# A one-core decoder layer: the first query block by token, squares at other places, one column more in the last sum

## The chip, the cores and the metric

The kernel runs on one core of one Trainium2 chip. The time is device microseconds of one launch on that core; the kernel before has a median of 2016.69 us over three runs (2016.46 to 2019.35). Lower is better. Besides the times there is one profiled execution, with the start and the length of every instruction on TensorE (PE, and PEld for its weight loads), VectorE (DVE), ScalarE (ACT) and GpSimd (POOL), the instructions that the SP queue issues, and the DMA transfers.

## The reference, cut to what matters

One decoder layer over 256 tokens of width 2048 in float32: two token mixers (retention and a gated recurrence) merged by gates, an attention over 256 memory rows, a gated feed-forward part, and a final normalisation.

```python
def rmsnorm(x, w):
    return x * lax.rsqrt(jnp.mean(x * x, axis=-1, keepdims=True) + 1e-6) * w

hn = rmsnorm(x, norm_mix_w)
q, k, v, g_ret, xr, yr, g_a, g_b = jnp.split(hn @ w_in, offsets, axis=-1)   # q, k: 1024 columns, the others 2048
q = rotary(q.reshape(b, s, 8, 128), positions)                               # turned by the token's position
k = rotary(k.reshape(b, s, 8, 128), positions) * 128 ** -0.5
ret = silu(g_ret) * head_groupnorm(chunkwise_retention(q, k, v), ret_gn_w)
rnn = gelu(yr) * rg_lru(causal_dwconv(xr, ...), ...)
merged = sigmoid(g_a) * (ret @ w_proj_ret) + sigmoid(g_b) * (rnn @ w_proj_rnn)
h = x + merged @ w_mix_out
h = h + memory_cross_attention(rmsnorm(h, norm_xa_w), rmsnorm(mem, norm_mem_w), ...)
h = h + conv_gated_ffn(rmsnorm(h, norm_ffn_w), ...)
return rmsnorm(h, final_norm_w)
```

## The kernel before, in words

**Products.** Every float32 product is made from parts: an operand is rounded to a high part `hi` (type fp32r) and the rest is the low part `lo`. Three products are summed, high by high, low by high and high by low. The weights come from one stream in memory, laid out in the order of use, in chunks of four k-tiles (128 rows each) by 512 columns, 1 MB; the first chunks of the first two products are of two k-tiles (`EARLY`). `prefetch` (L233) issues a chunk's load from the SP queue into a buffer `raw` (L249), of which there are three (`RAW_BUFS`), casts it to `hi` on ScalarE (L276; for the very first chunk on VectorE, L274) and subtracts for `lo` on VectorE (L277). The parts have six buffers of two k-tiles each, so that three chunks can be ready. `chunks` (L289) asks for two chunks ahead and, after each chunk, runs the functions that `later(n, fn)` put down for n chunks on. All matmuls keep the order in which they are written; the other instructions of each engine are put into an order by a planner, from the order of the text, priorities and its own estimate of when data are there. At run time each engine and each queue goes through its order strictly, waiting where something is not there.

**By token and by feature.** `steps_n` (L352) makes a product by token: a piece of the activations (128 x 128, of `xs`) is held in TensorE, and 512 weight columns stream past; the result has tokens on the partitions. Where features must be on the partitions, `turned_rows` (L401) copies the result out of PSUM (`rows`), and `by_dma` (L377) splits the words into halves on ScalarE (`pl`, L385), turns them with two DMA transposes from SP (`pt`, L387) and joins the halves on ScalarE (`f`, L396), some chunks later. `steps_t` (L312) makes a product by feature at once, with the weight piece held and the activations streaming: 512 columns (high and low) past `hi`, 256 (high) past `lo`. Only the first query block is made this way, into two PSUM accumulators; `joined` (L412) adds the two halves of each accumulator, and `rotated` (L589) applies the rotary tables. The first query block (`q_steps`) and the first value block (`v_steps`) take turns, chunk by chunk.

**The rows of x.** `Pairs` loads x by feature in pieces of two k-tiles (`xt`, L530) and splits them (`s`, L451 and L452). `load_x` (L223) loads x by token (`nat`), for the sums of squares that `sum_squares` (L488) makes on ScalarE while the chunks 8 and 9 are prefetched.

**Residual stages.** `residual` (L840) runs the products with `w_mix_out` and with `xa_w_o` in four blocks of 512 columns. For the first two blocks three chunks each are run ahead. After each block the rows of h are updated (L852), the squares are summed on ScalarE (`squares`, L867) and the rows are turned with `by_dma` for the next stage. In the `w_mix_out` stage `memory_steps` (L871) adds, ahead of block 1, the sums of squares of all four blocks of memory rows (`mnat`, eight instructions on ScalarE, L493).

**The tail.** `last_down` (L1012) makes the last 512 columns of the result, for each half of the tokens (`tt`) in two parts of 256 columns. Each part is added to the row and squared with a sum (L1025). VectorE then adds up the other sums and eps (L1030, L1031), adds the last one (L510), GpSimd raises to the power -0.5 (L512), and VectorE and ScalarE scale the rows, which go out by DMA.

Of the kernel before, what the change touches and what calls it, by code (L numbers as in the profile page):

```python
# [9 lines left out]
F32 = mybir.dt.float32  # L10
# [25 lines left out]
URGENT = 5  # L36
# [102 lines left out]
def hybrid_layer(  # L139
# [93 lines left out]
    def prefetch(n):  # L233
        while len(ahead) < n and taken[0] < len(stream):
# [6 lines left out]
            raw = wp.tile([P, KC, BW], F32, tag="raw", bufs=RAW_BUFS, name=nm("raw"))  # L241
# [12 lines left out]
            if i >= 5:  # L254
                load_x(min(4, i - 4))
# [56 lines left out]
    def steps_t(w, row, st, nk, col):  # L312

        accs = [acc(), acc()]
        first = gemms[0] == 0
        phase = 0
        for k0, n, parts in chunks(nk, w, row, col):
            last = k0 + n >= nk
            tiles = [(kk, j) for j in range(2) for kk in range(n)]
            if first and k0 == 0:  # L320
                runs = [[(t, pr, kk, j) for t in (0, 1)] for kk in range(n) for pr in range(2) for j in range(2)]
            elif last:
                runs = [[(t, pr, kk, j) for kk, j in tiles] for pr in range(2) for t in (1 - pr, pr)]
            else:
                runs = [[(t, pr, kk, j) for pr in range(2) for kk, j in tiles] for t in (phase, 1 - phase)]
                phase = 1 - phase
            for i, run in enumerate(runs):
                for t, pr, kk, j in run:
                    k = k0 + kk
                    sx = st[k // 2][:, k % 2, :]  # L330
                    part = parts[kk // KH][t][:, kk % KH, (2 * pr + j) * P : (2 * pr + j + 1) * P]
                    a = accs[pr][:, j, :]
                    if t == 1:
                        a, sx = a[:, S:BW], sx[:, 0:S]
                    mm(
                        a, part, sx, start=k == 0 and t == 0, stop=k == nk - 1 and t == 0, skip_group_check=True
                    )
                if i + 1 == len(runs) // 2 and not last and not first and isinstance(st, Pairs):
                    st[(k0 + n) // 2 + 1]
            yield accs  # L340

    def gemm_t(*args):
        return ended(steps_t(*args))

    def products_n(o, sx, hi, lo, tt, start, stop):
        h = sx[:, tt * P : (tt + 1) * P]
        l = sx[:, S + tt * P : S + (tt + 1) * P]
        mm(o, h, hi, start=start, stop=False)
        mm(o, l, hi, start=False, stop=False)
        mm(o, h, lo, start=False, stop=stop)  # L350

    def steps_n(w, row, st, nk, col):  # L352

        a = acc()
        for k0, n, parts in chunks(nk, w, row, col):
            for tt in range(2):
                for kk in range(n):
                    k = k0 + kk
# [52 lines left out]

    def joined(a, s="j"):  # L412

        c = tmp("c")
        o = tmp(s)
        with tc.high_priority(URGENT):
            act.copy(c, a[:, :, S:BW])
            dve.tensor_tensor(out=o, in0=a[:, :, 0:S], in1=c, op=ALU.add)
        return o
# [121 lines left out]
    q_steps = steps_t("w_in", 0, xs, NT, O_Q)  # L541
# [41 lines left out]
    qjoin = [joined(t, "q") for t in next(q_steps)]  # L583
    assert next(q_steps, None) is None
# [87 lines left out]
    for g in range(2):  # L672
        dec = big([P, 4, S], s="dec")
        vs, turned = [], ([], [])
        for b, o in enumerate((O_Q, O_K)):
            if g + b:
                def rotate_both(f, o=turned[b]):
                    o.append(rotated(f[:, 0:2, :]))
                    later(0, lambda: o.append(rotated(f[:, 2:4, :])))
# [160 lines left out]
    def residual(w, st, out, wcol, steps=None):  # L840
# [3 lines left out]
        for b in range(4):  # L844
# [8 lines left out]
            squares(h, ss, b)  # L853
            by_dma(hrow[b], lambda f, b=b: turn(f, b, out, wcol))
# [157 lines left out]
    def last_down(b0, hid, n, b):  # L1012
        h = hrow[b]
        accs = [acc(), acc()]
        parts = [p for _, _, ps in chunks(n, "ffn_w_down", b0 * BW, b * BW) for p in ps]
        for tt in range(2):
            for c in range(2):
                cs = slice(c * S, (c + 1) * S)
                for k in range(n):
                    hi, lo = (t[:, k % KH, cs] for t in parts[k // KH])  # L1020
                    products_n(accs[c][:, tt, 0:S], hid[k // 2][:, k % 2, :], hi, lo, tt, k == 0, k == n - 1)
                y = h[:, tt, cs]
                dve.tensor_add(y, y, accs[c][:, tt, 0:S])
                junk = tp.tile([P, S], F32, tag="tr", bufs=2, name=nm("junk"))
                dve.scalar_tensor_tensor(  # L1025
                    out=junk, in0=y, scalar=1.0, in1=y, op0=ALU.mult, op1=ALU.mult,
                    accum_out=ss3[:, tt, b + c : b + c + 1],
                )
            part = sp_.tile([P, 1], F32, tag="pt3", bufs=2, name=nm("pt3"))
            dve.tensor_reduce(out=part, in_=ss3[:, tt, 0:4], axis=AX.X, op=ALU.add)  # L1030
            dve.tensor_scalar(out=part, in0=part, scalar1=1.0 / D, scalar2=EPS, op0=ALU.mult, op1=ALU.add)  # L1031
            r = rsqrt_small(ss3[:, tt, 4:5], 1, 1.0 / D, part)
            for c in (1, 0, 3, 2):
                y = hrow[c][:, tt, :]
                if c == 3:
                    dve.scalar_tensor_tensor(
                        out=y, in0=y, scalar=r, in1=wfin[1][:, 1, :], op0=ALU.mult, op1=ALU.mult
# [70 lines left out]
```

## Time and profile before

| what | value |
|---|---|
| median of three runs | 2016.69 us |
| the profiled execution's own time | 2016.58 us |
| its span | 2014.5 us |
| mean granted TensorE clock | 0.997 |
| TensorE busy | 1999.1 us |
| ScalarE, VectorE busy | 1247.8, 1263.5 us |
| GpSimd busy | 7.7 us |
| DMA, mean | 210 GB/s |
| TensorE idle, 60 us to the end, until `hi` | 2.5 us, once |
| the same, until `lo`, until `s` | 0.5 us, once each |

The span runs from the first to the last instruction of the trace; the time of the run has 2.08 us more. Matmuls are pipelined, so a single matmul of 512 columns is shown as 0.39 us long while the next one starts 0.227 us after it; intervals from start to start are read, not lengths. A line of the timeline that stands for several instructions shows their number (x16), the start of the first and the time to the end of the last. The granted clock in the windows is the share of full speed that TensorE was given.

### The profile page before, as it was taken

How to read it: one execution, taken by the hardware profiler on the slowest of the kernel's cores; microseconds unless marked ns; L12 is line 12 of the kernel's file. 1: busy time of each engine (PE TensorE's matmuls, PEld its weight loads, DVE VectorE, ACT ScalarE, POOL GpSimd, SP SyncE). 2: the span in 40 equal slices, each digit the busy share in tenths (PEclk: the TensorE clock that was granted, in tenths of full speed). 3: DMA queues.
4: the chain of work that ended last, by engine and by line, in shares of the span. 5: the costliest groups of instructions: out<-in, count | busy, mean ns of one | idle time of the engine just before them, and what ended most of it. 6: DMA issues, size and time to landing. Idle time of an engine off the chain costs nothing.

```text
span 2014.5 us, 23604 instructions
## 1 busy us (share of the span) xinstructions
PE 1999.1 (99%) x9044; PEld 1664.3 (83%) x9044; DVE 1263.5 (63%) x1563; ACT 1247.8 (62%) x1506; POOL 7.7 (0%) x12
## 2 busy tenths in 40 slices
PE   9999999999999999999999999999999999999998
PEld 7888888888888888878888888888888888888887
DVE  5867757888545555456555555566775577664675
ACT  5556648888444455487675656766763466744763
POOL 0000000000000000000000000000000000000000
PEclk9999999999999999999999999999999999999999
DMA  8755757665555566767766645767665566655663
GB/s 299 233 210 172 235 199 196 235 206 188 209 190 192 195 207 211 260 227 241 227 208 205 197 176 184 217 205 215 214 223 216 195 191 217 232 210 200 208 230 125
DMA packets 189376, 423.02 MB, mean 210 GB/s; under 512 B 131664, under 2 KB 136400, under 8 KB 144208
## 3 DMA queue, kind: packets, MB, share of 16 engines
q1 hardware_dynamic: 188832, 421.00, 63.5%
q8 instruction: 70, 1.15, 0.2%
q10 hardware_dynamic: 432, 0.53, 0.1%
q14 instruction: 42, 0.34, 0.0%
HBM read 388.46 MB, written 2.10 MB: 194 GB/s over the span
## 4 chain that ended last, share of the span: by engine, by line
PE 96%; DMA 1%; ACT 1%; issue 1%; DVE 1%; SPq 0%; POOLq 0%; POOL 0%; ACTq 0%; DVEq 0%
PE acc L214 94%; PE sm L214 3%; DMA raw<-in_wall 1%; DMA pt<-pl 1%; DVE lo L277 0%; ACT pl L385 0%; ACT hi L276 0%; ACT f L396 0%; ACT junk L867 0%; DVE nat L852 0%; ACT s L451 0%; SPq L249 0%; ACT nat L1042 0%; DVE s L452 0%; SPq L387 0%
## 5 line engine op out<-in xcount | busy, mean ns | idle before, releaser
L214 PE MATMUL acc<-hi,s 128*128 128x512 f32 (+1 forms) x5680 | 1739.9, 388 | 3.0 <-ACT hi L276 2.5
L277 DVE TENSOR_TENSOR lo<-raw,hi 128x1024 fp32r<-128x1024 f32 (+1 forms) x714 | 859.4, 1218 | 645.9 <-ACT hi L276 629.5
L214 PEld LDWEIGHTS acc<-hi,s 128*128 128x128 f32 x5680 | 1062.4, 188 | 220.1 <-ACT hi L276 2.9
L214 PE MATMUL acc<-lo,s 128*128 128x512 f32 (+1 forms) x2840 | 1100.6, 388 | 0.5 <-DVE lo L277 0.5
L276 ACT CAST hi<-raw 128x1024 fp32r<-128x1024 f32 (+1 forms) x712 | 733.0, 1048 | 497.5 <-PE acc L214 428.1
L214 PEld LDWEIGHTS acc<-lo,s 128*128 128x128 f32 x2840 | 533.7, 188 | 110.1 <-DVE lo L277 1.0
L396 ACT COPY f<-pt 128x1024 uint16<-128x1024 uint16 x118 | 151.4, 1349 | 85.0 <-DMA pt<-pl 85.0
L385 ACT COPY pl<-rows 128x1024 uint16<-128x1024 uint16 x90 | 89.7, 1044 | 64.5 <-DVE rows L409 55.8
L409 DVE TENSOR_SCALAR rows<-acc,ro 128x512 f32<-128x512 f32 x68 | 47.7, 742 | 3.1 <-PE acc L214 3.1
L965 DVE SCALAR_TENSOR_TENSOR fv<-f,pf,fv 128x255 f32<-128x255 f32 (+1 forms) x88 | 35.8, 477 | 0.7 <-ACT fv L963 0.7
L965 DVE SCALAR_TENSOR_TENSOR fg<-f,pf,fg 128x255 f32<-128x255 f32 (+1 forms) x88 | 35.6, 477 | 0.0
L452 DVE SCALAR_TENSOR_TENSOR s<-f,pb,s 128x256 fp32r<-128x256 f32 x48 | 20.1, 478 | 6.6 <-ACT s L451 6.6
L963 ACT ACTIVATE fv<-f,pf 128x256 f32<-128x256 f32 x44 | 22.9, 592 | 0.0
L963 ACT ACTIVATE fg<-f,pf 128x256 f32<-128x256 f32 x44 | 22.8, 591 | 0.0
L428 ACT ACTIVATE s<-fo 128x512 fp32r<-128x512 f32 x22 | 13.6, 633 | 14.2 <-DVE fo L985 14.2
L777 DVE SCALAR_TENSOR_TENSOR xr<-f,pa,xr 128x255 f32<-128x255 f32 (+2 forms) x48 | 19.9, 478 | 3.1 <-ACT xr L775 3.0
L451 ACT ACTIVATE s<-f,pb 128x256 fp32r<-128x256 f32 x48 | 20.6, 498 | 0.0
L385 ACT COPY pl<-nat 128x1024 uint16<-128x1024 uint16 x16 | 15.9, 1042 | 6.9 <-DVE nat L852 6.9
L214 PEld LDWEIGHTS sm<-s,s 128*128 128x128 f32 x144 | 18.8, 191 | 0.9
L214 PE MATMUL sm<-s,s 128*128 128x256 f32 (+1 forms) x144 | 18.6, 279 | 0.0
L214 PE MATMUL acc<-s,hi 128*128 128x512 f32 x64 | 17.4, 410 | 0.4 <-DVE hi L274 0.3
L440 ACT ACTIVATE v<-acc,ro 128x512 fp32r<-128x512 f32 x16 | 10.9, 683 | 7.7 <-DVE v L441 7.7
(152 smaller groups left out, 625.5 us busy)
## 6 DMA issues: line engine op xcount, KB each, us to landing
raw<-in_wall SPq DMA_DIRECT2D x352, 1024.0 KB, 4.8
nat<-in_x SPq DMA_DIRECT2D x8, 512.0 KB, 7.8
raw<-in_wall SPq DMA_DIRECT2D x6, 512.0 KB, 6.8
nat<-in_mem SPq DMA_DIRECT2D x4, 512.0 KB, 9.3
xt<-in_mem_t SPq DMA_DIRECT2D x8, 256.0 KB, 3.6
pt<-pl SPq DMA_TRANSPOSE x118, 4.1
xt<-in_x_t SPq DMA_DIRECT2D x7, 256.0 KB, 8.2
out<-nat SPq DMA_DIRECT2D x6, 256.0 KB, 2.8
```

Source lines behind the costliest of these rows:

```text
L214: tc.keep_in_program_order(pe.matmul(*a, **k))
L276: act.copy(hi[:, ds], raw[:, cs, :])
L277: dve.tensor_tensor(out=lo[:, ds], in0=raw[:, cs, :], in1=hi[:, ds].bitcast(F32), op=ALU.subtract)
L385: act.copy(planes[:, :, h, :], words[:, h])
L396: act.copy(halves_[:, h], turned_[:, h])
L409: dve.tensor_scalar_mul(rows[:, tt, :], a[:, tt, :], r[:, tt : tt + 1])
L428: act.mul(t[:, :, 0:S], src, scale)
L451: act.activation(t[:, j, 0:S], src[:, j, :], AF.Identity, scale=wcol(j))
L452: dve.scalar_tensor_tensor(out=t[:, j, S:BW], in0=src[:, j, :], scalar=wcol(j), in1=t[:, j, 0:S].bitcast(F32), op0=ALU.mult, op1=ALU.subtract,
L777: dve.scalar_tensor_tensor(out=y[:, s:S], in0=z[:, 0 : S - s], scalar=p_cw(3 - s, t), in1=y[:, s:S], op0=ALU.mult, op1=ALU.add,)
L963: act.activation(y, z[:, j, :], AF.Identity, scale=pf[:, 2, t : t + 1], bias=pf[:, 3, t : t + 1])
L965: dve.scalar_tensor_tensor(out=y[:, s:S], in0=z[:, j, 0 : S - s], scalar=pf[:, 2 - s, t : t + 1], in1=y[:, s:S], op0=ALU.mult, op1=ALU.add,)
```

## The change

The first query block is made by token like the others, with `steps_n`, and turned by DMA, three chunks after its end; `steps_t` and `joined` are gone. In the very first chunk the two halves of the tokens take turns, so that four products with `hi` come before two with `lo`. The first four weight chunks are loaded into tiles of the big pool (27 buffers) instead of the three `raw` buffers. The loads of x by token start with chunk 6 instead of 5.

In `residual` the turn is put ahead of the squares, block 1 is turned one chunk later, and the squares of blocks 0 and 1 are made some chunks later. The sums of squares of the memory rows are made one block per chunk from the start of the `w_mix_out` stage.

In `last_down` the new rows go to a tile `last` with one column more. GpSimd puts the root of all sums but the last one there (with eps), and the last square and sum run over 257 columns with a factor 1/2048, so that the sum is already the whole mean with eps, and GpSimd's power follows it directly.

```diff
@@ prefetch @@
-            raw = wp.tile([P, KC, BW], F32, tag="raw", bufs=RAW_BUFS, name=nm("raw"))
+            if i < 4:
+                raw = big([P, KH, BW], s="raw")
+            else:
+                raw = wp.tile([P, KC, BW], F32, tag="raw", bufs=RAW_BUFS, name=nm("raw"))
...
-            if i >= 5:
-                load_x(min(4, i - 4))
+            if i >= 6:
+                load_x(min(4, 2 * i - 11))
@@ steps_t is taken out, products_n and steps_n @@
         mm(o, h, hi, start=start, stop=False)
         mm(o, l, hi, start=False, stop=False)
+        yield
         mm(o, h, lo, start=False, stop=stop)
+        yield
...
+            if first and k0 == 0:
                 for kk in range(n):
-                    k = k0 + kk
-                    hi, lo = (t[:, kk % KH, :] for t in parts[kk // KH])
-                    products_n(a[:, tt, :], st[k // 2][:, k % 2, :], hi, lo, tt, k == 0, k == nk - 1)
-                if tt == 0 and isinstance(st, Pairs):
-                    st[min(NT, k0 + 3 * n) // 2 - 1]
+                    for _ in zip(*(tile_(tt, kk) for tt in range(2))):
+                        pass
+            else:
+                for tt in range(2):
+                    for kk in range(n):
+                        for _ in tile_(tt, kk):
+                            pass
+                    if tt == 0 and isinstance(st, Pairs):
+                        st[min(NT, k0 + 3 * n) // 2 - 1]
@@ the first blocks @@
-    q_steps = steps_t("w_in", 0, xs, NT, O_Q)
+    q_steps = steps_n("w_in", 0, xs, NT, O_Q)
...
-    qjoin = [joined(t, "q") for t in next(q_steps)]
-    assert next(q_steps, None) is None
+    q0 = ended(q_steps)
...
-                turned_rows(gemm_n("w_in", 0, xs, NT, o + g * BW), None, rotate_both, 2 - b)
+            a = gemm_n("w_in", 0, xs, NT, o + g * BW) if g + b else q0
+            turned_rows(a, None, rotate_both, 2 - b if g + b else 3)
...
-            if g + b == 0:
-                turned[0].extend(rotated(q) for q in qjoin)
@@ residual and memory_steps @@
-            squares(h, ss, b)
-            by_dma(hrow[b], lambda f, b=b: turn(f, b, out, wcol))
+            by_dma(h, lambda f, b=b: turn(f, b, out, wcol), 1 + (b == 1))
+            if b < 2:
+                later(2 + b, lambda h=h, b=b: squares(h, ss, b))
+            else:
+                squares(h, ss, b)
...
-        if b == 1:
+        if b == 0:
             ss = sums()
             for c in range(4):
-                sum_squares(mnat[c], ss, c)
-            rsms.append(rstd_rows(ss))
+                later(c, lambda c=c: sum_squares(mnat[c], ss, c))
+            later(4, lambda: rsms.append(rstd_rows(ss)))
@@ last_down @@
+            last = big([P, BW + 1], s="last")
+            before = sp_.tile([P, 1], F32, tag="pt3", bufs=2, name=nm("pt3"))
...
-                y = h[:, tt, cs]
-                dve.tensor_add(y, y, accs[c][:, tt, 0:S])
+                y = last[:, c * S : (c + 1) * S + c]
+                dve.tensor_add(last[:, cs], h[:, tt, cs], accs[c][:, tt, 0:S])
...
-                    out=junk, in0=y, scalar=1.0, in1=y, op0=ALU.mult, op1=ALU.mult,
+                    out=junk[:, 0 : S + c], in0=y, scalar=1.0 / D if c else 1.0, in1=y, op0=ALU.mult, op1=ALU.mult,
...
-            part = sp_.tile([P, 1], F32, tag="pt3", bufs=2, name=nm("pt3"))
-            dve.tensor_reduce(out=part, in_=ss3[:, tt, 0:4], axis=AX.X, op=ALU.add)
-            dve.tensor_scalar(out=part, in0=part, scalar1=1.0 / D, scalar2=EPS, op0=ALU.mult, op1=ALU.add)
-            r = rsqrt_small(ss3[:, tt, 4:5], 1, 1.0 / D, part)
+                if c == 0:
+                    dve.tensor_reduce(out=before, in_=ss3[:, tt, 0:4], axis=AX.X, op=ALU.add)
+                    dve.tensor_scalar_add(before, before, EPS * D)
+                    pool.tensor_tensor(out=last[:, BW : BW + 1], in0=before, in1=half, op=ALU.pow)
+            r = sp_.tile([P, 1], F32, tag="ro", bufs=5, name=nm("ro"))
+            pool.tensor_tensor(out=r, in0=ss3[:, tt, 4:5], in1=mhalf[:, 0:1], op=ALU.pow)
```

More of the change, by code (lines that the diff above doesn't have):

```diff
@@ L35 @@
 WARM = 8
-URGENT = 5
 FREE = 300
@@ L310, in ended @@
         return a
[L312 to L328, printed above, removed]
-                    k = k0 + kk
[L330 to L343, printed above, removed]
     def products_n(o, sx, hi, lo, tt, start, stop):
@@ L349, in products_n, with tile_ @@
         mm(o, l, hi, start=False, stop=False)
+        yield
         mm(o, h, lo, start=False, stop=stop)
+        yield
     def steps_n(w, row, st, nk, col):
         a = acc()
+        first = gemms[0] == 0
         for k0, n, parts in chunks(nk, w, row, col):
-            for tt in range(2):
-                for kk in range(n):
-                    k = k0 + kk
-                    hi, lo = (t[:, kk % KH, :] for t in parts[kk // KH])
-                    products_n(a[:, tt, :], st[k // 2][:, k % 2, :], hi, lo, tt, k == 0, k == nk - 1)
-                if tt == 0 and isinstance(st, Pairs):
-                    st[min(NT, k0 + 3 * n) // 2 - 1]
+            def tile_(tt, kk):
+                k = k0 + kk
+                hi, lo = (t[:, kk % KH, :] for t in parts[kk // KH])
+                return products_n(a[:, tt, :], st[k // 2][:, k % 2, :], hi, lo, tt, k == 0, k == nk - 1)
+            if first and k0 == 0:
+                for kk in range(n):
+                    for _ in zip(*(tile_(tt, kk) for tt in range(2))):
[7 more added lines that the diff above has]
+                        st[min(NT, k0 + 3 * n) // 2 - 1]
             yield a
@@ L410, in turned_rows @@
         by_dma(rows, then, wait)
[L412 to L419, printed above, removed]
     def split_pair(src, scale=None):
@@ L675, in hybrid_layer, with rotate_both @@
         for b, o in enumerate((O_Q, O_K)):
[L676 to L679, printed above, removed]
-                turned_rows(gemm_n("w_in", 0, xs, NT, o + g * BW), None, rotate_both, 2 - b)
+            def rotate_both(f, o=turned[b]):
+                o.append(rotated(f[:, 0:2, :]))
+                later(0, lambda: o.append(rotated(f[:, 2:4, :])))
+            a = gemm_n("w_in", 0, xs, NT, o + g * BW) if g + b else q0
+            turned_rows(a, None, rotate_both, 2 - b if g + b else 3)
             if b == 1:
@@ L1013, in last_down @@
         h = hrow[b]
+        half = sp_.tile([P, 1], F32, tag="half", bufs=1, name="half")
+        dve.memset(half, 0.5)
         accs = [acc(), acc()]
@@ L1036, in last_down @@
                     dve.scalar_tensor_tensor(
-                        out=y, in0=y, scalar=r, in1=wfin[1][:, 1, :], op0=ALU.mult, op1=ALU.mult
+                        out=y, in0=last[:, 0:BW], scalar=r, in1=wfin[1][:, 1, :], op0=ALU.mult, op1=ALU.mult
                     )
```

5 lines of the change are left out of this document (3 added, 2 removed).

## The prediction

> **What bounds the kernel now.** I read the page first: which engine is full.
>
> ```profile
> PE 1999.1 (99%) x9044; PEld 1664.3 (83%) x9044; DVE 1263.5 (63%) x1563; ACT 1247.8 (62%) x1506; POOL 7.7 (0%) x12
> PE 96%; DMA 1%; ACT 1%; issue 1%; DVE 1%; SPq 0%; POOLq 0%; POOL 0%; ACTq 0%; DVEq 0%
> ```
>
> TensorE is busy for 99% of the span and is 96% of the chain, so the time is its matmuls plus its few gaps. Next I read its timeline, at the three places where the chain of waits leaves it: the start, the end of the `w_mix_out` stage, and the tail. A weight chunk of four k-tiles is 24 matmuls of 512 columns; when nothing is late one follows another every 0.227 us (5.44 us a chunk).
>
> ```profile
> 4.68 0.47 PE L214 MATMUL acc<-s,hi 128*128 128x512 f32 x1
> ...
> 18.33 0.50 PE L214 MATMUL acc<-s,lo 128*128 128x256 f32 x2 [0.99 <-DVE lo L277]
> 20.27 2.62 PE L214 MATMUL acc<-s,lo 128*128 128x256 f32 x14 [1.44 <-DVE lo L277]
> 22.70 4.73 PE L214 MATMUL acc<-s,hi 128*128 128x512 f32 x16
> ...
> 32.71 3.79 PE L214 MATMUL acc<-s,hi 128*128 128x512 f32 x16
> 36.34 2.08 PE L214 MATMUL acc<-s,lo 128*128 128x256 f32 x16
> ...
> 49.28 0.60 PE L214 MATMUL sm<-diag,ones 128*128 128x128 f32 x4
> ```
>
> Columns: start, length, engine, line, operation, tiles, count, and in brackets the idle time before it and who ended it. The first product starts at 4.68; between 17.2 and 20.3 it waits twice for a low part (`lo`); then sixteen matmuls take 4.57 us (22.70 to 27.27), against 3.63 us from 32.71 on. In the windows the granted clock is 0.60 at 21 us and 0.50 at 22 and 23. The next view is TensorE and then ScalarE around 880 us.
>
> ```profile
> 877.50 0.39 PE L214 MATMUL acc<-lo,s 128*128 128x512 f32 x1
> 880.37 0.73 PE L214 MATMUL acc<-hi,s 128*128 128x512 f32 x2 [2.48 <-ACT hi L276]
> 881.63 0.79 PE L214 MATMUL acc<-lo,s 128*128 128x512 f32 x1 [0.53 <-DVE lo L277]
> 882.22 1.05 PE L214 MATMUL acc<-hi,s 128*128 128x512 f32 x2
> ```
>
> ```profile
> 865.39 0.63 ACT L867 ACTIVATE junk<-nat 128x512 f32<-128x512 f32 x1
> ...
> 876.38 1.98 ACT L385 COPY pl<-nat 128x1024 uint16<-128x1024 uint16 x2
> 878.26 0.50 ACT L451 ACTIVATE s<-f,pb 128x256 fp32r<-128x256 f32 x1
> 878.67 0.61 ACT L867 ACTIVATE junk<-nat 128x512 f32<-128x512 f32 x1
> 879.29 3.87 ACT L276 CAST hi<-raw 128x1024 fp32r<-128x1024 f32 x4
> ```
>
> TensorE waits for `hi`, which ScalarE casts only at 879.29, after ten squares in a row from 865.39 to 871.6 (eight of them of the memory rows, L493) and another ahead of block 1's turn (`pl` at 876.38). The windows show ScalarE 10.00 of 10 us busy from 876 to 886, and a clock of 0.50 from 882 to 884. Last, VectorE and GpSimd at the tail:
>
> ```profile
> 2007.61 0.08 DVE L1025 DVE_READ_ACCUMULATOR junk<-nat 128x1 f32 x1
> 2007.73 0.21 DVE L510 TENSOR_SCALAR rv<-ss,pt 128x1 f32<-128x1 f32 x1
> 2008.02 0.55 POOL L512 TENSOR_TENSOR ro<-rv,mhalf 128x1 f32<-128x1 f32 x1 [8.00 <-DVE rv L510]
> ```
>
> The profiled run took 2016.58 us, 2.08 over its span and 0.11 under the median of 2016.69; the sum is made from 2016.58.
>
> **Part 1, the first query block and its weights.** Matmul columns do not change: before, 64 of 512 and 64 of 256 columns; after, 96 of 512. Sixteen of 256 take 1.91 us (36.34 to 38.25), 0.119 each, so 64 x 0.119 = 7.64 us become 32 x 0.227 = 7.25: 0.4 us gained. Up to the small products at 49.28 the kernel runs nine chunks (query 64 + 64, value 72): 136 x 0.227 + 7.64 = 38.5 us of matmuls in 49.28 - 4.68 = 44.6 us. So 6.1 us are lost there. After the change they are 168 x 0.227 = 38.1 us.
>
> I replay them with the trace's own arrival times. Chunk 0's first k-tile: four products with `hi`, then two with `lo`, which is ready at 5.26, so the wait of 0.4 us there goes; six end at 6.04. The second k-tile's first matmul was at 7.03, and `hi` is no earlier: a wait of 0.99. Chunk 0 ends at 8.39 and chunk 1 (2.72 us) at 11.11. Chunk 2 is the query's again; before it ran all its `hi` products first, now each tile needs `lo` after two, and `lo` was done at 12.29: two matmuls, a wait of 0.76, ten more, end at 14.59. Chunk 3 ends at 17.31. Chunk 4 was the one that began with `lo` and stood; now it begins with `hi`. Its `lo` halves were done at 18.28 and 20.22, which would leave waits of 0.55 and 0.58. But its loads were issued at 9.29 and 10.13, as the three raw buffers came free; with four first chunks in the big pool SP issues them without that wait. From 11 to 14 us the windows show 172 to 193 GB/s, from 15 to 20 us over 400: moving the same 2.5 MB at 400 from 10 us on lands them near 16.3 instead of 17.9. Both waits are shorter than that, so I take none. Five chunks of 5.44 end at 44.5: 4.8 us gained. Bounds: 3.7 with the old arrivals, less 1.9 if the new waits cost one clock drop (below), so 1.8; at best no wait at all, 49.28 - 4.68 - 38.1 = 6.5.
>
> What the turn adds: two PSUM copies on VectorE (0.681 each) for two additions (0.687), nothing; on ScalarE two `pl` (1.044) and two `f` (1.348) less two `c` (0.587), 3.6 us. They are hidden: ScalarE stands 6.4 us before 46.71 and is 4.75 of 10 us busy from 60 to 70. Gone with this cover they would delay casts, which are made up to two chunks (11 us) early. The rotations move from 64 us to the chunk ending near 66, out of a stretch where VectorE is 9.86 of 10 busy; scores that read them come after 140 us. Two transposes go through SP (rival 4). Loads of `x` rows start one chunk later and two `xt` loads come one chunk earlier: up to chunk 7 the same bytes. One accumulator less is held: no wait for it was seen, zero.
>
> **Part 2, squares.** From 877.50 to 888.01 there are 24 matmuls and 5.07 us more than 24 x 0.227: idle 2.64 and 0.53, the other 1.9 half clock. The eight squares of the memory rows (8 x 0.615 = 4.9 us) go to the end of the first four chunks of the stage, and those of blocks 0 and 1 (2 x 1.24) behind later chunks. Without them ScalarE reaches block 1's `pl` some 6 us earlier, SP's transposes (which held SP from 865.5 to 881.0) and the `hi` cast with it; that cast came about 2.6 us too late. From 844.4 ScalarE stood 6.69 us for a weight load, room for the eight squares. What is late next: the `xa_w_o` stage runs the same loop without memory squares, and its only gap is 0.48 us at 1303.98, in the last block's turn, which does not change. I take 5.07; bounds 0 (the cast is late for another reason) and 5.07. Block 1's turn one chunk later: its tiles are read four chunks on, zero. The squares of the `xa_w_o` stage: no matmul waited for them, zero.
>
> **Part 3, the tail.** After the last sum VectorE's 0.21 us and the 0.04 ahead of it go: GpSimd can start at 2007.77 instead of 2008.02, 0.25 gained. The added root (0.55 on GpSimd) can start at about 2003.9, after the first half's sum, is read at 2007.26, and GpSimd's last power stands behind it: 2.8 us to spare, hidden. VectorE's square of the second half now waits for it, with only the scaling queued behind. Bounds 0 and 0.4 (with one more hand-over).
>
> Sum: 4.8 + 5.07 + 0.25 = 10.1; 2016.58 - 10.1 = 2006.5.
>
> **A rule against a row.** The clock fell to 0.50 at 882 after a gap of 2.64 us, and at 22 us after idle times of 1.0 and 1.4. The other way, chunk 0's three waits of about 0.4 us within 3 us left it at 1.00. The Trainium skill, TensorE: Matmul & The Clock Gate, section "HAM oscillation — how this bites in real kernels", gives "no PE-idle gaps >~3.4µs" as the limit. By that page no drop could follow here, part 1's lower bound would be 3.7 and its value the same; the trace disagrees at 2.64 us. From the rows I keep 1.9 us (5.07 less 3.2 idle) as the price of a drop.
>
> **Rivals.**
> 1. The gap at 880 us stays or moves: the memory rows, issued from 835.24 on with 9.3 us to landing, are not there when the first squares come up in ScalarE's order near 830, and casts stand behind them. For: ScalarE works in order. Against: casts have 11 us of slack, and ScalarE idles later. Part 2 then gives nothing: 2016.58 - 4.8 - 0.25 = 2011.5.
> 2. The start is bound by transfers: the windows show DMA 0.94 busy even from 11 to 13 us, so earlier issue moves nothing, and new waits cost a drop or two. Part 1 gives 0.4: 2010.9.
> 3. Neither stall goes, as casts only change places: 0.4 + 0.25, 2015.9.
> 4. Slower: SP stands at the first block's transposes while the weights behind them (chunk 11) wait. Rows are ready at 45.9; in the `w_mix_out` stage block 1's `pl` came 8.1 us after its rows, and the transposes were issued 4.6 us after it started. Then the load leaves at 58.6, lands 4.8 later (the page's median), casts take 2.3: 65.7, and chunk 11 was due at 55.4. A gap of 10.3 and a drop of 1.9 outweigh the gain: 2018.7; with the 7.26 us that SP held the key block's transposes at 81.16, 2021.3. It decides once that load leaves after 56.5. Against: SP idles there, and the weights can be issued ahead.
>
> **How the numbers follow.** The forecast has 0.58, rival 1 0.12, rival 2 0.11, rival 3 0.08, rival 4 0.11. About 0.2%, 4.0 us, is what a measurement of this kernel tells from no change, so faster means under 2012.7. That holds the forecast, and most of rivals 1 and 2 (0.16): 0.74. The same: the rest of these two, rival 3 and a third of 4, 0.18. Slower, over 2020.7: 0.08. The range runs from 2004.6 (2016.58 less the upper bounds 6.5, 5.07 and 0.4) to 2012.5, which takes in rivals 1 and 2: 0.81 together.
>
> **What would show it.** Matmuls up to the small products end near 44.5; no clock under 1.00 around 22 us; chunk 4 without a gap. Around 878 no wait for `hi`, the memory squares before 851. At the tail GpSimd 0.1 us after the last sum. Wrong if the clock still falls at either place, if SP waits for `pl` near 45 to 56 us, or if VectorE, full from 50 to 80 us, lets a `lo` come late.

## The result and the profile after

The changed kernel takes 2013.88 us in the median of 22 runs (2009.70 to 2015.88). The kernel before took 2016.47 beside it (22 runs, 2014.03 to 2023.29). The ratio is 0.9984, with a 95% interval of 0.9977 to 0.9990: some 3 us gained, where 10 were forecast, and outside the range. The profiled run took 2014.38 us with a span of 2012.6; before it was 2016.58 and 2014.5.

The first two lines that were shown of the page before, here of the page after, say nothing of it:

```profile
PE 1999.2 (99%) x9012; PEld 1663.0 (83%) x9012; DVE 1263.7 (63%) x1562; ACT 1251.5 (62%) x1508; POOL 8.8 (0%) x14
PE 96%; ACT 1%; DMA 1%; DVE 1%; issue 1%; SPq 0%; POOL 0%; POOLq 0%; DVEq 0%; ACTq 0%
```

TensorE is as full as it was. Where the time went is read from four marks on the timeline that both kernels have: the small products (`sm<-diag`), the first scores product, the first softmax product (`sm<-s,s x24`) and the last addition of the tail. The stretches between them, in us of each profiled execution, with those of the experiments that follow (the spans are given to 0.1 us, so the last column is good to about 0.05):

| kernel | start to small products | to first scores | to softmax | to last addition | to the span's end |
|---|---|---|---|---|---|
| before | 49.28 | 98.38 | 833.06 | 1026.08 | 7.70 |
| after | 45.80 | 98.95 | 834.88 | 1025.30 | 7.67 |
| p1_only | 45.83 | 98.95 | 833.05 | 1025.63 | 7.84 |
| p2_only | 49.01 | 98.38 | 829.73 | 1026.99 | 7.79 |
| ms_early | 45.63 | 98.92 | 827.98 | 1027.40 | 7.67 |
| no_bigraw | 45.75 | 98.92 | 834.80 | 1025.77 | 7.66 |
| p2_ms | 47.14 | 98.38 | 827.99 | 1026.53 | 7.76 |
| before_ms | 47.89 | 98.38 | 836.15 | 1026.34 | 7.74 |
| mem_sq | 47.41 | 98.38 | 829.89 | 1029.89 | 7.73 |
| ms_rows | 44.63 | 98.40 | 827.98 | 1025.31 | 7.68 |
| after_again | 45.87 | 98.92 | 834.42 | 1026.88 | 7.61 |
| sq_back | 45.70 | 98.96 | 833.83 | 1025.83 | 7.58 |
| ms_rows_2 | 44.89 | 98.40 | 827.98 | 1026.68 | 7.65 |

Between the first two rows 3.48 us are gained at the start, 0.57 lost behind it, 1.82 lost up to the softmax, 0.78 gained after it and 0.03 at the end: 1.90, the difference of the spans. The third stretch holds the `w_mix_out` stage, where 5.07 were to be gained. Four kernels show what it takes when nothing there is late: 827.98 or 827.99.

The changed kernel's TensorE at the start and behind the small products:

```profile
4.61 2.04 PE L213 MATMUL acc<-hi,s 128*128 128x512 f32 x4
6.45 0.88 PE L213 MATMUL acc<-lo,s 128*128 128x512 f32 x2
...
12.21 0.73 PE L213 MATMUL acc<-hi,s 128*128 128x512 f32 x2 [0.45 <-ACT hi L278]
13.47 0.50 PE L213 MATMUL acc<-lo,s 128*128 128x512 f32 x1 [0.53 <-DVE lo L279]
...
45.80 0.61 PE L213 MATMUL sm<-diag,ones 128*128 128x128 f32 x4
...
48.47 0.50 PE L213 MATMUL acc<-lo,s 128*128 128x512 f32 x1 [0.22 <-DVE lo L279]
```

The two waits between 17 and 20 us and the half clock behind them are gone; the windows from 17 to 24 us show a clock of 1.00. What is left are small waits: the first four products take 1.84 us instead of 0.91, and chunk 2 stands twice for its parts. A new wait for `lo` appears at 48.47.

The next view is the same engine at 878 and at 918 us. At 878, where the kernel before stood, no matmul waits. Forty microseconds on:

```profile
918.11 0.39 PE L213 MATMUL acc<-lo,s 128*128 128x512 f32 x1
920.70 0.50 PE L213 MATMUL acc<-hi,s 128*128 128x512 f32 x1 [2.20 <-ACT s L424]
922.48 0.79 PE L213 MATMUL acc<-hi,s 128*128 128x512 f32 x1 [1.28 <-DVE s L425]
923.07 0.63 PE L213 MATMUL acc<-lo,s 128*128 128x512 f32 x1
923.49 1.05 PE L213 MATMUL acc<-hi,s 128*128 128x512 f32 x2
```

Two matmuls of 512 columns should start 0.453 us before the next; from 923.49 they take 0.86. The windows (busy us and count of PE, PEld, DVE, ACT and POOL, then the granted clock, the DMA share and GB/s) show half clock:

```profile
922.00:924.00 2.00, 1.52 (x4) 1.24 (x5) 2.00 (x6) 1.73 (x2) 0.00 (x0) 0.50 1.14 272
924.00:926.00 2.00, 2.00 (x6) 1.57 (x5) 2.00 (x3) 0.93 (x3) 0.00 (x0) 0.50 1.11 304
926.00:928.00 2.00, 2.00 (x6) 1.55 (x5) 1.46 (x4) 2.00 (x4) 0.00 (x0) 0.50 0.96 389
```

Against 827.98 this stretch loses 6.90 us: 3.48 idle, the other 3.4 half clock. The releaser `s` is a memory tile, scaled on ScalarE and completed on VectorE. This is the third chunk of the product of the memory rows with `xa_w_k`, which needs the tiles 4 and 5. ScalarE there, after and then before:

```profile
915.12 2.00 ACT L367 COPY pl<-nat 128x1024 uint16<-128x1024 uint16 x2 [1.83 <-DVE nat L823]
917.02 0.63 ACT L841 ACTIVATE junk<-nat 128x512 f32<-128x512 f32 x1
...
917.64 0.62 ACT L841 ACTIVATE junk<-nat 128x512 f32<-128x512 f32 x1
...
918.26 1.98 ACT L278 CAST hi<-raw 128x1024 fp32r<-128x1024 f32 x2
920.14 1.70 ACT L424 ACTIVATE s<-xt,pb 128x256 fp32r<-128x256 f32 x4
```

```profile
918.15 2.00 ACT L385 COPY pl<-nat 128x1024 uint16<-128x1024 uint16 x2 [1.69 <-DVE nat L852]
...
923.18 1.71 ACT L451 ACTIVATE s<-xt,pb 128x256 fp32r<-128x256 f32 x4
```

The order is the same: block 3's copies (`pl`), two squares, two casts, then the four `s`. The whole group moved from 918.15 to 915.12, that is 3 us earlier, and VectorE's part in the kernel before is this:

```profile
924.98 1.66 DVE L452 SCALAR_TENSOR_TENSOR s<-xt,pb,s 128x256 fp32r<-128x256 f32 x4
```

TensorE in the kernel before comes to that chunk without a wait:

```profile
926.32 0.61 PE L214 MATMUL acc<-hi,s 128*128 128x512 f32 x2
```

Half of VectorE's part, the first tile, was done near 925.8, and TensorE came at 926.32: half a microsecond to spare. After, TensorE comes at 918.34, 8.0 us earlier (2.91 from the start and 5.07 from the gap at 878), and finds tiles that moved by 3.

At the tail (VectorE, then GpSimd):

```profile
2005.46 0.43 DVE L1005 SCALAR_TENSOR_TENSOR junk<-last 128x257 f32<-128x257 f32 x1
2005.81 0.08 DVE L1005 DVE_READ_ACCUMULATOR junk<-last 128x1 f32 x1
```

```profile
2002.10 0.54 POOL L1012 TENSOR_TENSOR last<-pt,half 128x1 f32<-128x1 f32 x1 [4.21 <-DVE pt L1011]
2005.97 0.54 POOL L1014 TENSOR_TENSOR ro<-ss,mhalf 128x1 f32<-128x1 f32 x1 [3.33 <-DVE junk L1005]
```

From the start of the last addition (2004.93) to GpSimd's last power (2005.97) it is 1.04 us; before it was 2006.80 to 2008.02, 1.22. The added root is done at 2002.64, far ahead of the square that reads it.

### The profile page after: what moved, and what is told of

Its sections match the earlier page's. It is cut to its first block, busy times and chain, and to the rows that moved or that the text cites. A ratio compares the mean times of both kernels' runs of the same rounds, so it can differ in the third digit from the quotient of the medians.

```text
span 2012.6 us, 23552 instructions
## 1 busy us (share of the span) xinstructions
PE 1999.2 (99%) x9012; PEld 1663.0 (83%) x9012; DVE 1263.7 (63%) x1562; ACT 1251.5 (62%) x1508; POOL 8.8 (0%) x14
## 4 chain that ended last, share of the span: by engine, by line
PE 96%; ACT 1%; DMA 1%; DVE 1%; issue 1%; SPq 0%; POOL 0%; POOLq 0%; DVEq 0%; ACTq 0%
PE acc L213 94%; PE sm L213 3%; DMA raw<-in_wall 0%; DVE lo L279 0%; DMA pt<-pl 0%; SPq L369 0%; ACT s L424 0%; ACT f L378 0%; DVE s L425 0%; DMA xt<-in_mem_t 0%; ACT hi L278 0%; ACT junk L841 0%; DVE nat L823 0%; ACT pl L367 0%; SPq L251 0%
## 5 line engine op out<-in xcount | busy, mean ns | idle before, releaser
L213 PE MATMUL acc<-hi,s 128*128 128x512 f32 (+1 forms) x5744 | 1761.5, 388 | 3.9 <-ACT s L424 2.2
L213 PEld LDWEIGHTS acc<-hi,s 128*128 128x128 f32 x5744 | 1075.5, 188 | 224.5 <-ACT s L424 2.6
L213 PE MATMUL acc<-lo,s 128*128 128x512 f32 (+1 forms) x2872 | 1113.7, 388 | 0.7 <-DVE lo L279 0.7
L213 PEld LDWEIGHTS acc<-lo,s 128*128 128x128 f32 x2872 | 540.2, 188 | 112.8 <-DVE lo L279 2.0
L398 ACT CAST s<-ta 128x512 fp32r<-128x512 f32 x8 | 5.0, 622 | 18.4 <-DVE ta L571 18.4
```

What stands on the lines that cost most here:

```text
L213: tc.keep_in_program_order(pe.matmul(*a, **k))
```

## The experiments

The runs stand in three groups, each on a chip of its own (`p1_only` to `no_bigraw`, `p2_ms` to `ms_rows`, and the last three), and each beside its own runs of the kernel before. Between groups the ratios are to be compared, not the times.

Two theories stood at the outset. **A**: the chain that makes the memory tiles is late for `xa_w_k`, since the planner leaves tiles 4 and 5 behind block 3's work on ScalarE; made earlier, the stall goes. **B**: ScalarE's work in this stage is conserved, and a stall removed at one place has to come back at another.

**Each part by itself.** `p1_only` is the changed kernel with the `residual`, `memory_steps` and `last_down` of before; `p2_only` is the kernel before with the changed `residual` and `memory_steps`.

```diff
 # p1_only, against the changed kernel
-            if b < 2:
-                later(2 + b, lambda h=h, b=b: squares(h, ss, b))
...
+            squares(h, ss, b)
+            by_dma(hrow[b], lambda f, b=b: turn(f, b, out, wcol))
```

> Part 1 alone (first query block by token, first weights in the big pool), squares and tail as before. Theory A (the gap of the changed kernel at 918 us comes from the memory tiles for the third chunk of xa_w_k, which stand behind the last block's turn on ScalarE) and theory B (ScalarE simply has too much work from 860 to 920 us, so that a gap taken away there comes back) agree here: the gap of about 5 us at 875 us stays, the one at 918 us does not appear, and the kernel is 2.5 to 3.5 us faster than before, what the changed kernel has won by 145 us of its span.

> Part 2 alone (squares at their new places). Both theories: the gap at 878 us goes (5.1 us) and one of 5 to 7 us appears near 921 us, at the third chunk of xa_w_k; with the 0.6 us at 1304 us it comes to -1 to +2 us against before. The forecast's reading (nothing late next) would give -5 us.

Measured, against a kernel before of 2014.92 (27 runs): `p1_only` 2013.15, ratio 0.9989 [0.9980, 0.9998], 1.8 us by the medians where 2.5 to 3.5 were expected; `p2_only` 2014.64, ratio 1.0001 [0.9992, 1.0010]. In the trace of `p1_only` TensorE still stands at 877 us:

```profile
877.27 0.73 PE L213 MATMUL acc<-hi,s 128*128 128x512 f32 x2 [2.26 <-ACT hi L278]
878.53 0.50 PE L213 MATMUL acc<-lo,s 128*128 128x512 f32 x1 [0.53 <-DVE lo L279]
```

`p2_only` has lost that gap, and near 920 it has one small one without half clock:

```profile
922.80 0.51 PE L214 MATMUL acc<-hi,s 128*128 128x512 f32 x1 [1.27 <-DVE s L452]
```

The gap near 920 was expected at 5 to 7 us; the whole stretch is only 1.75 us over 827.98. So the size of the new stall hangs on part 1. Block 1's features (`f`) on ScalarE, in the changed kernel and in `p2_only`:

```profile
883.26 2.56 ACT L378 COPY f<-pt 128x1024 uint16<-128x1024 uint16 x2 [3.33 <-DMA pt<-pl]
```

```profile
883.62 2.57 ACT L396 COPY f<-pt 128x1024 uint16<-128x1024 uint16 x2 [1.06 <-DMA pt<-pl]
```

From there to the four `s` (920.14 and 920.47) both take 36.9 us. With part 1 TensorE is some 2.7 us earlier, and so is ScalarE at block 0's copies (860.59 against 863.23); at block 1's copies 2.0 us of that lead are left (874.50 against 876.54), at block 1's features 0.36. The lead is lost at the DMA transposes: those of block 1 land 5.4 to 5.9 us after their issue in the changed kernel, 3.7 to 4.2 in `p2_only`. TensorE keeps its lead and waits. Why the transposes take longer there was not tested. The profile of `p2_only` shows 3.3 us less up to the softmax than that of the kernel before, which is not of this group; its median shows no gain. That difference is not explained.

**The memory tiles one block earlier.** `ms_early` is the changed kernel with one character changed.

```diff
     def memory_steps(b):
...
-        if b == 3:
+        if b == 2:
             ms.load(2)
```

> The changed kernel with the loads and splits of the memory rows by feature asked for one block earlier (ahead of block 2 instead of block 3 of the w_mix_out stage). Theory A: no gap at 918 us, 5 to 7 us faster than the changed kernel, near 2007.5. Theory B: the same work on ScalarE, so a gap of 4 us or more stays somewhere between 860 and 930 us, and the time is within 2 us of the changed kernel.

Measured: 2007.47, ratio 0.9966 [0.9952, 0.9979], 6.4 us under the changed kernel's median and 7.1 under `no_bigraw` on the same chip; by the ratios (0.9966 against 0.9984) it is 3.6. The stretch takes 6.90 us less. From 860 to 930 us no matmul waits. ScalarE of `ms_early` at the place:

```profile
909.49 2.00 ACT L367 COPY pl<-nat 128x1024 uint16<-128x1024 uint16 x2 [1.21 <-DVE nat L823]
...
914.51 1.71 ACT L424 ACTIVATE s<-xt,pb 128x256 fp32r<-128x256 f32 x4
```

The four `s` stand at 914.51 instead of 920.14, ahead of need. ScalarE has the same instructions to run, so B falls.

A holds in its main point, that the memory tiles are late, but not in its reason. The tiles 4 and 5 have not changed places: block 3's copies, two squares and two casts still stand ahead of them, and the whole group moved by 5.6 us. What changed places are the tiles 0 to 3, eight `s` on ScalarE. They begin like this in the changed kernel and in `ms_early`:

```profile
901.99 0.91 ACT L424 ACTIVATE s<-xt,pb 128x256 fp32r<-128x256 f32 x2 [3.10 <-DMA xt<-in_mem_t]
```

```profile
875.03 1.70 ACT L424 ACTIVATE s<-xt,pb 128x256 fp32r<-128x256 f32 x4
```

In the changed kernel they stand between block 2's and block 3's copies, and ScalarE waits 3.10 us for the first of them to land. VectorE, which completes them, adds block 3's rows (L823) only at 913.87, though by the count of matmuls (two chunks of 24 ahead of 918.34) TensorE was through with that block near 907.5. In `ms_early` it adds them at 908.24.

**The big pool at the start.** `no_bigraw` is the changed kernel with all raw weights in their three buffers.

```diff
-            if i < 4:
+            if i < 0:
                 raw = big([P, KH, BW], s="raw")
```

> The changed kernel with all raw weights in the three raw buffers, as before. If transfers issued early take speed from those ahead of them, the second and third chunks land as before (ScalarE's casts at 7.9 and 9.97 us instead of 8.5 and 11.1), the first gaps shrink by about 1 us, and gaps of 0.5 us each come at the fifth chunk: within 1 us of the changed kernel. If transfers land in the order of issue at the pace of the engines, the first casts stay late and the fifth chunk's loads are 1.5 us later: 1 to 2 us slower.

Measured: 2014.55, ratio 0.9995 [0.9987, 1.0004]; small products at 45.75 against 45.80. The first raw weights in the big pool are worth nothing that shows here, and chunk 4 has no gap without them either. The first casts of landed weights (7.07, 9.10 and 11.07) stand as late as in the changed kernel, against 6.84, 7.91 and 9.97 before, and chunk 4's second cast is 1.5 us later than in the changed kernel (17.75 against 16.25). That is the second case of the expectation, but the 1 to 2 us of loss that it gave did not come. TensorE begins chunk 4 here at 18.55, 1.36 us later than before (17.19), and begins it with `hi`; which of the two removed the gap no run shows.

**Is part 1 worth anything once nothing eats it?** `p2_ms` is `p2_only` with the memory tiles one block earlier, so that against `ms_early` only parts 1 and 3 are missing.

```diff
 # against p2_only
-        if b == 3:
+        if b == 2:
```

> Part 2 alone with the memory tiles turned one block earlier (b == 2); the first query block is the old one. Theory A (part 1 is worth its 2.9 us, but in the changed kernel they are spent waiting for the memory tiles): no gap between 870 and 930, first scores product near 147.5, last addition near 2002.9, that is 2.9 later than with both changes (1999.93), and a time of about 2010.4, ratio near 0.998. Theory C (part 1 is worth nothing to the end, the 6 us come from the memory tiles alone): the same time as with both, about 2007.5, ratio near 0.9966.

Measured: 2010.57, ratio 0.9977 [0.9968, 0.9986], against 2015.72 for the kernel before (27 runs; the same for the next three). The stall near 920 is gone and part 2 gives 833.06 - 827.99 = 5.07 us, all that was forecast. Against 0.9966 for `ms_early`, parts 1 and 3 are then worth about 0.0011, 2.2 us; the two intervals overlap, so this leans to A and does not settle against C alone. `p1_only` (0.9989) says the same size. The profile leans the other way: the last addition comes at 2000.04, not near the 2002.9 expected, and only 0.11 us after that of `ms_early`, as C would have it. Its start took 1.51 us longer, but the stretch up to the first scores 0.54 and the one after the softmax 0.87 less, and that last one varies by more from profile to profile.

**The memory tiles alone.** `before_ms` is the kernel before with that one edit.

```diff
 # against the kernel before
-        if b == 3:
+        if b == 2:
```

> The kernel before with the memory tiles turned one block earlier and nothing else. Theory A (the stall at 878 us comes from the squares of the memory rows, and had covered the late memory tiles): the stall stays, 4 to 6 us of loss between 870 and 890, no other gap up to 930, time as before within 1.5 us. Theory D (the early memory tiles are worth 6 us by themselves, whatever the squares do): 6 us faster, about 2009.

Measured: 2017.75, ratio 1.0011 [1.0003, 1.0020]: slower. The gap at 878 stays (2.81 us idle, for `hi`), and a second one of 1.29 stands behind 926, where tiles 4 and 5 come at 925.78, later than the 923.18 of before. D falls. The edit that gains 6 us in the changed kernel costs about 2 where the squares still hold ScalarE up; "no other gap" was missed by that 1.29, and "as before within 1.5 us" by the 2.0 of the medians.

**Which squares?** `mem_sq` is the kernel before with only the squares of the memory rows spread; `sq_back` is the changed kernel with the blocks' squares and turn as before.

```diff
 # mem_sq, against the kernel before
-        if b == 1:
+        if b == 0:
             ss = sums()
             for c in range(4):
-                sum_squares(mnat[c], ss, c)
-            rsms.append(rstd_rows(ss))
+                later(c, lambda c=c: sum_squares(mnat[c], ss, c))
+            later(4, lambda: rsms.append(rstd_rows(ss)))
```

```diff
 # sq_back, against the changed kernel
-            by_dma(h, lambda f, b=b: turn(f, b, out, wcol), 1 + (b == 1))
-            if b < 2:
-                later(2 + b, lambda h=h, b=b: squares(h, ss, b))
-            else:
-                squares(h, ss, b)
+            squares(h, ss, b)
+            by_dma(hrow[b], lambda f, b=b: turn(f, b, out, wcol))
```

> The kernel before with only the squares of the memory rows spread over the first chunks of the stage; the blocks' own squares and the turn of block 1 as before. If those eight squares are what held block 1's turn, the gap at 878 us is gone and one of at most 2 us, without half clock, stands near 920 as with the whole of part 2: 1 to 4 us faster in the profile than before. If it was the blocks' own squares and the turn's place, the gap at 878 stays at 4 to 6 us and the time is that of the kernel before.

> The changed kernel with the squares of the blocks' rows and the turn of block 1 back in their old places; the squares of the memory rows, the first query block and the tail stay changed. On ScalarE the planner gives the four squares of blocks 0 and 1 the same places, between block 0's two copies and block 1's, whichever way they are written. So this half of part 2 is worth nothing: the time of the changed kernel within 1.5 us, and the same gap near 918. If it cost something (the changed memory squares alone seemed better than all of part 2: 0.9986 against 1.0001), this kernel is 2 to 3 us faster than the changed one.

> The changed kernel once more, on the chip of the two kernels beside it. Theory A: the gap near 918 us is there again, 5 to 7 us of loss with the clock at half behind it, as TensorE again comes to the third chunk some 8 us earlier than in the kernel before. If its size wanders from run to run (two other kernels showed 1.5 us there), it may be as small as 2; the ratio to before stays between 0.997 and 0.9995.

Measured: `mem_sq` 2012.28, ratio 0.9986 [0.9977, 0.9994], with no wait at 878 and 1.28 us at 921. So the eight memory squares alone held block 1's turn. Then, against a kernel before of 2016.51 (21 runs): `sq_back` 2013.70, ratio 0.9989 [0.9980, 0.9997]; the changed kernel once more 2014.21, ratio 0.9991 [0.9982, 1.0000]. The two are the same. ScalarE of `sq_back`, between block 0's copies and block 1's:

```profile
860.49 1.99 ACT L367 COPY pl<-nat 128x1024 uint16<-128x1024 uint16 x2 [1.06 <-DVE nat L823]
862.39 0.63 ACT L838 ACTIVATE junk<-nat 128x512 f32<-128x512 f32 x1
...
863.02 0.62 ACT L838 ACTIVATE junk<-nat 128x512 f32<-128x512 f32 x1
...
865.52 0.63 ACT L838 ACTIVATE junk<-nat 128x512 f32<-128x512 f32 x1
...
866.14 0.62 ACT L838 ACTIVATE junk<-nat 128x512 f32<-128x512 f32 x1
```

and of the changed kernel, where they were to come two and three chunks later:

```profile
860.59 2.00 ACT L367 COPY pl<-nat 128x1024 uint16<-128x1024 uint16 x2 [1.06 <-DVE nat L823]
862.49 0.63 ACT L841 ACTIVATE junk<-nat 128x512 f32<-128x512 f32 x1
...
865.00 0.63 ACT L841 ACTIVATE junk<-nat 128x512 f32<-128x512 f32 x1
...
865.63 0.61 ACT L841 ACTIVATE junk<-nat 128x512 f32<-128x512 f32 x1
...
866.24 0.62 ACT L841 ACTIVATE junk<-nat 128x512 f32<-128x512 f32 x1
```

Three of the four stand within about 0.1 us of the same places and one two casts later, all of them still ahead of block 1's copies: the planner has its own idea of when they fit, however they are written, and that half of part 2 does nothing in this stage. The stall near 920 is in every profile that has the memory squares spread and the tiles at their old time: the stretch is 1.7 to 1.9 us over 827.98 with the old start (`p2_only`, `mem_sq`) and 5.9 to 6.9 over it with the new one (after, `after_again`, `no_bigraw`, `sq_back`).

**The copies behind the small products.** VectorE ran the two copies of the first query block's rows (1.29 us from 46.00, in the changed kernel) ahead of a `lo` that TensorE wanted at 48.1. `ms_rows` is `ms_early` with these copies at no priority.

```diff
-    def turned_rows(a, r, then, wait=1):
+    def turned_rows(a, r, then, wait=1, front=FREE):
...
-        with tc.high_priority(FREE):
+        with tc.high_priority(front):
...
-            turned_rows(a, None, rotate_both, 2 - b if g + b else 3)
+            turned_rows(a, None, rotate_both, 2 - b if g + b else 3, FREE if g + b else 0)
```

> The changed kernel with the memory tiles one block earlier, and the two copies of the first query block's rows without their high priority, so that the second low part of the chunk there stands ahead of them on VectorE. Expected: no wait for lo between 46 and 49 us (0.39 lost there before), first scores product 0.4 to 0.6 earlier than 144.55, and the end likewise: about 2007.0. If the rows then come so late that the weights behind their transposes wait, a gap shows near 55 us.

> The best kernel so far (memory tiles one block earlier, rows copies of the first block without priority) beside the changed kernel on one chip. Theory A: 6 to 7 us faster than the changed kernel, ratio to before near 0.996, no gap from 860 to 930 us.

Measured: 2006.86, ratio 0.9958 [0.9945, 0.9970], the first time; 2007.58, ratio 0.9960 [0.9947, 0.9972], beside the changed kernel and 6.6 us under it, the second. This is the best version here. From the small products to the first scores it takes 98.40 us in both, against 98.92 to 98.96: 0.52 to 0.56 gained, as expected, and no wait for `lo` there. VectorE of `ms_rows`:

```profile
44.83 1.29 DVE L389 COPY rows<-acc 128x512 f32<-128x512 f32 x2 [2.71 <-PE acc L213]
46.03 0.28 DVE L543 TENSOR_SCALAR rot<-rot 128x256 f32<-128x256 f32 x1
46.63 2.36 DVE L279 TENSOR_TENSOR lo<-raw,hi 128x1024 fp32r<-128x1024 f32 x2 [0.31 <-ACT hi L278]
```

One `lo` now goes ahead of the copies, at 40.9 us, and the next two are ready in time. The small products themselves also came about 1 us earlier (44.63 and 44.89). Up to 40.9 us the instructions have the same order as in `ms_early` on every engine, and VectorE's `diag` already stands 0.99 us earlier there (38.70 against 39.69), so the edit is not the reason; it is the spread of the start, below.

## Why the prediction was wrong, step by step

**What bounds the kernel** held: TensorE and its few gaps. All that was gained or lost lies in gaps.

**Part 1, forecast 4.8, measured 3.48 in the profiled pair and 2.85 to 3.4 on two other chips, less 0.57.** Right: the gap at chunk 4 and the clock drop behind it went, and the small columns were of no matter. Three terms were mis-sized.
- The base. The old start takes 49.28, 49.01, 47.14, 47.89 and 47.41 us in five profiles; the profile before happened to be the longest. The first two had a clock drop at 21 us, the other three had none. "6.1 us are lost there" was read from one execution. The three short ones all ran on one chip, so a mean over all would mix the chips. On that chip the changed start takes 44.63, 2.85 less than their mean of 47.48; on the chip of `p2_only` (49.01) it takes 45.63 to 45.83, 3.2 to 3.4 less.
- The waits. The replay had 1.75 us of them (0.99 and 0.76); the changed kernel has 3.1 (45.80 - 4.61 - 38.1). The first four products, for which it had none, lose 0.93, and chunk 2 loses 1.4. It took the old arrival times, and the loads of the first weights land at other times in each execution: the first cast on ScalarE of a landed weight started at 6.84 before, and at 7.39, 8.32, 8.34, 6.60 and 6.29 in after, `after_again`, `ms_early`, `ms_rows` and `ms_rows_2`, which start with the same order of work.
- "With four first chunks in the big pool SP issues them without that wait" was of no consequence: chunk 4 has no gap with the three buffers either (`no_bigraw`).

"Two PSUM copies ... for two additions ..., nothing" failed too: the copies cost VectorE the same time, but they stand ahead of a `lo` that was just on time. `ms_rows` priced that at 0.52 to 0.56.

**Part 2, forecast 5.07, measured -1.82 in the profiled pair.** The mechanism and the size were right: with the memory tiles out of the way part 2 gives 5.07 to the hundredth (`p2_ms`), and the memory squares do it (`mem_sq`). The step that failed is "What is late next", with its lower bound of 0: no term stood for a stall that the gain itself brings out. It looked for the next late thing in the `xa_w_o` stage, which runs the same loop but makes no memory tiles, and not forty microseconds further down this stage. There the tiles had half a microsecond to spare, and they had it because of the very gap that the change removes. The blocks' own squares, which part 2 counted among what goes "behind later chunks", hardly move.

**Part 3, forecast 0.25, measured 0.18**: VectorE's square starts 0.11 us after the addition now instead of 0.04. From the last addition to the end of the span it is 7.76 us in the mean of the six profiles with the old tail and 7.65 in the seven with the new one, about 0.1.

**The rule against the row.** The row won: after idle times of 2.20 and 1.28 us with one matmul between them the clock was 0.50 from 922 to 928. The Trainium skill, TensorE: Matmul & The Clock Gate, section "HAM oscillation — how this bites in real kernels", sets its limit at gaps above about 3.4 us; neither gap is that long, and their sum is 3.48. In `before_ms` a single idle time of 2.81 us was enough: the clock was 0.50 from 879 on, and TensorE came back at 879.31. The price of a drop, 1.9 us in the prediction, is loss less idle: 6.90 - 3.48 = 3.4 in the changed kernel, 5.85 - 3.68 = 2.2 in `sq_back` for the same stall.

**The rivals.** Rival 1 said that the gap stays or moves. It did move, but for the memory tiles that the next stage reads, not for the memory rows that the squares read: ScalarE waited 2.51 us for those rows at 840 and nothing came of it. Rival 2 fell: no new wait brought a clock drop in the eight profiles with the changed start, and that start gained 2.85 us or more, not 0.4. Rival 3's time, 2015.9, was nearest and its mechanism was not the one: the first stall went. Rival 4 did not come: SP issues the first block's transposes and has the next weights out at 54.06, before the 56.5 from which it would have decided.

```profile
49.35 4.61 SPq L369 DMA_TRANSPOSE pt<-pl  x2
54.06 0.52 SPq L251 DMA_DIRECT2D raw<-in_wall  x1
```

That a tile read later in the stage has no more slack than the gap gives it was not among the rivals; with the stall as measured it would have given 2006.5 + 6.9 = 2013.4.

## What to carry to other kernels

Before a stall is booked as gained, take every later tile of the same stage that the bound engine reads, and note how long before its use it was ready: what had less slack than the stall is the next stall, and if it stands behind other work on an engine that keeps its order, that work is to be moved in the same edit. An edit that clears the way for such a tile can be worth nothing, or cost time, before the first stall is gone (here +2 us) and most of the gain after it (here -6). Size a start from several executions, and compare them on one chip, for it spreads by as much as a small change gains.

## What the runs showed of the hardware that was not expected

- The start differs by 2.1 us between executions with the same order of work at the start (47.14 to 49.28), with a clock drop in the two longest alone. The three shortest are of one chip, and on one chip it spreads by 0.2 to 1.0 us (45.63 to 45.83, 47.14 to 47.89, 44.89 to 45.87); whether the rest is the chip or chance no run parts. The first loads land at other times even on one chip: first cast at 8.32, 6.77 and 6.29 in `after_again`, `sq_back` and `ms_rows_2`. What makes them do so stays open.
- Two short waits can cost a clock drop or not. With idle times of 0.77 and 1.42 us, two matmuls apart, the granted clock fell to 0.50 (`p2_only`, first line); with 0.38 and 1.42 it stayed at 1.00 (`p2_ms`, second line).

```profile
22.00:23.00 1.00, 1.00 (x5) 0.90 (x4) 0.52 (x1) 0.19 (x1) 0.00 (x0) 0.50 0.98 403
```

```profile
22.00:23.00 1.00, 1.00 (x6) 0.83 (x5) 0.88 (x3) 0.74 (x2) 0.00 (x0) 1.00 0.99 404
```

- A single wait of 1.27 to 1.29 us left the clock at 1.00 (`p2_only`, `mem_sq`, `before_ms`); the same wait right behind one of 1.73 to 2.41 did not (after, `after_again`, `no_bigraw`, `sq_back`).
- The stretch after the softmax, which no experiment touched but for its squares, varied from 1025.30 to 1029.89 us, with waits for a low part in six of the thirteen profiles; 2 us between two single profiles prove nothing there.
